# A decoder layer in fp32: gate and up of the ffn wholly by seven products, with new raw buffers and queued sums

## The chip, the cores and the metric

The kernel runs on one core of a Trainium2 chip, in one launch. The metric is the device time of the launch in microseconds (us), the median of three runs. TensorE (PE) multiplies; its weight loads are listed apart as PEld and overlap the products. VectorE (DVE), ScalarE (ACT) and GpSimd (POOL) are the elementwise engines, and SyncE (SP) issues most transfers from HBM.

## The reference

One layer of a decoder for 256 tokens of width 2048, all in float32: a half-step ffn, a mixer of attention and gated linear attention, cross attention into 256 memory tokens, and a second half-step ffn. What matters here are the two ffns, of hidden width 5632:

```python
def swiglu(h, w_gate, w_up, w_down):
    return (jax.nn.silu(h @ w_gate) * (h @ w_up)) @ w_down

x = x + 0.5 * swiglu(rms_norm(x, ffn1_norm), ...)      # the same again at the end, with ffn2's weights
```

## The kernel before, in words

**Numbers.** An fp32 product is made of three fp32r matmuls: each operand is split into a rounded high part and the rest, and high x high, high x low and low x high are summed in one PSUM bank. A weight tile of 128 x 4 x 512 floats (1 MB) is loaded raw by SP, ScalarE casts it to `wh` in two halves (L157 or L201), DVE subtracts for `wl` (L158 or L202), and PE multiplies. The pools of `wh` and `wl` have four halves each (`WB`), so DVE runs at most four halves ahead of PE. x stands transposed in four chunks `xT[c]` of 4 K-tiles, each as a high and a low tile.

**The ffn.** The hidden width is cut in 11 blocks f of 512 columns. For each f, gate and up are formed (two token tiles of 128 each, so four PSUM banks), silu(gate) * up goes to `sg` on DVE (L216, as every `urgent` operation), it is transposed by PE into hT (`turn`, L387; `hTh` on ScalarE, `hTl` on DVE L304), and `down` multiplies it by four 512-column chunks of w_down, 24 matmuls each, banks `dn`, adding to the residual `xs`. The downs of f-1 are put between the steps of f.

**Seven products.** f=0 forms gate and up plainly, 96 matmuls each. From f=1 on, gate and up of one f are treated together as a 2 x 2 block product: x's two token tiles by two K-parts, times K-parts by (gate, up). `seven` (L257) computes it with seven block products for eight, in the banks Y, Z, X and R: sums of weight blocks, T = gate + gate', T + up and so on, are formed on raw tiles by DVE (`add`, L207) or by an accumulating transfer that POOL issues (`add_hbm`, L211), and the differences of x blocks (`xf`, `d`, `Fh`, `Fl`) are formed once for each ffn by `x_differences` (L400) and kept. Before, chunks 0 and 1 are one pair of blocks (four K-tiles), the two halves of chunk 2 are a second pair (two K-tiles), and chunk 3 is plain: 84 + 42 + 48 = 174 matmuls for each f. The differences are put off by `later(DIFF, ...)` into up of f=0; the rest of them comes at the change to f=1.

**Order.** Each engine runs its instructions in one order, which the framework sets from the order in the code and from priorities (`high_priority`): a larger number goes earlier as far as its operands and buffers allow. Loads have `LPRI`, splits and sums `WPRI`, the steps that free a bank `FPRI`.

**Buffers.** Raw tiles come from a pool for the whole kernel (4 x 1 MB), and in the ffns from two more (`r`, 3 x 1 MB, and `q`, 4 halves). `enter` closes the pools of a stage and opens those of the next. A buffer of the pool for the whole kernel passes from one stage to the next by itself; one in a pool of the stage starts when the old pool is done.

Of the kernel before, what the change touches and what calls it, by code (L numbers as in the profile page):

```python
# [8 lines left out]
F32 = mybir.dt.float32  # L9
# [7 lines left out]
P = 128  # L17
# [13 lines left out]
WARM = 10  # L31
# [12 lines left out]
UF = 18  # L44
UM = 34
SB = 7
RB = 4
RX = 3
RQ = 4
DIFF = 1  # L50
# [3 lines left out]
def layer_kernel(ctx: ExitStack, tc: tile.TileContext, A: dict, out: bass.AP):  # L54
# [25 lines left out]
    def enter_ffn():  # L80
        enter(2, down=2, u=UF, r=RX, q=RQ)

# [3 lines left out]
    def raw_tile(kind="raw"):  # L86

        if kind == "raw":
            return wp.tile([P, 4, 512], F32, tag="raw", name="raw", bufs=RB)
        return stage[kind].tile([P, 2 if kind == "q" else 4, 512], F32, tag=kind, name="raw")  # L90
# [45 lines left out]

    def wgroup(W, c, g, fine=None):
# [4 lines left out]
        with tc.high_priority(WPRI):  # L142
            if wload:
                raw = wload.pop(0)
            else:
                raw = wp.tile([P, kn, n], F32, tag="raw", name="raw", bufs=RB)
                SY.dma_start(raw, W[c, g])
        for h in range(2):
            with tc.high_priority(WPRI):
                wh = wp.tile([P, m, n], F32R, tag="wh", name="wh", bufs=WB)  # L150
                wl = wp.tile([P, m, n], F32R, tag="wl", name="wl", bufs=WB)
                for i in range(m if fine else 1):
# [5 lines left out]
                    V.tensor_sub(wl[:, d], src, wh[:, d].bitcast(F32))  # L158
# [29 lines left out]
    def load(src, kind="raw"):  # L188
        with tc.high_priority(ahead[0]):
            raw = raw_tile(kind)  # L190
            SY.dma_start(raw, src)
        return raw

    def parts(raw, n=4):

        for h in range(n // 2):
            with tc.high_priority(WPRI):
# [4 lines left out]
                V.tensor_sub(wl, src, wh.bitcast(F32))  # L202
            yield [(2 * h + kk, wh[:, kk], wl[:, kk]) for kk in range(2)]

    def add(dst, src):
        with tc.high_priority(WPRI):
            V.tensor_add(dst, dst, src)  # L207

    def add_hbm(dst, src):
        with tc.high_priority(WPRI):  # L210
            G.dma_start(dst, src, accum_op=ALU.add)  # L211
# [13 lines left out]
    def product(bank, form, raw, start, n):  # L225

        for h, half in enumerate(parts(raw, n)):
            mms(bank, form, half, start and h == 0, h == n // 2 - 1)
# [8 lines left out]
    PAIRS = {"22-21": ((1, 1), (1, 0)), "12-21": ((0, 1), (1, 0)), "22-12": ((1, 1), (0, 1)),  # L237
             "21-11": ((1, 0), (0, 0)), "11-12": ((0, 0), (0, 1))}

    def difference(x, name, n, home=None):  # L240

        a, b = PAIRS[name]
        with tc.high_priority(WPRI):
            d = W2([P, n, P], "d")
            V.tensor_sub(d, x[a], x[b])
            if home:
                hi, lo = home
            elif n == 4:
                hi, lo = (U([P, 4, P], F32R, nm) for nm in ("Fh", "Fl"))
            else:  # L250
                both = U([P, 4, P], F32R, "Fhl")
                hi, lo = both[:, 0:2], both[:, 2:4]
            SC.copy(hi, d)
            V.tensor_sub(lo, d, hi.bitcast(F32))
        return hi, lo

    def seven(blocks, ld, last, rest):  # L257
# [22 lines left out]
        for i, (n, kinds, F, A12, A21) in enumerate(blocks):  # L280
            b22.append(load(ld(i, 1, 1), kinds[3]))
            add(T[i], b22[i])
            product(R, A12, T[i], i == 0, n)
        urgent(V.tensor_sub, X, R, sw)
# [6 lines left out]
        urgent(V.tensor_sub, R, R, sv)  # L291
        for i, (n, kinds, F, A12, A21) in enumerate(blocks):
            product(X, F["22-12"], b22[i], False, n)
        plain((R, X), (rest(0), rest(1)), load(last(1)), (1, 0))
        yield "down"
        for i, (n, kinds, F, A12, A21) in enumerate(blocks):
            product(Y, F["11-12"], b12[i], False, n)
        yield "down"
        plain((Y, Z), (rest(0), rest(1)), load(last(0)), (0, 1))
        return Y, Z, R, X  # L300
# [817 lines left out]
```

## Time and profile before

| | |
|---|---|
| Median of three runs | 1919.39 us (1917.73 to 1922.42) |
| The profiled execution's own time | 1917.25 us |
| Its span | 1915.5 us |
| Granted TensorE clock, mean | 0.998 |
| PE busy | 1892.8 us (99%) |
| DVE busy | 1471.9 us (77%) |
| ACT busy | 1288.9 us (67%) |
| POOL busy | 94.8 us (5%) |

The span runs from the first to the last instruction of the profiled execution; its own time has some 2 us around it. An engine's busy time is a mean over stages: the loop of the ffns takes about seven tenths of the span and is alike in each period from f=2 on. Matmul records overlap, so their pitch (start to start) is what one costs, not their length.

### The profile page before, as it was taken

To read this page: it belongs to the slowest core of one execution; us is meant where nothing else is said; L and a number is where in the kernel's file an instruction comes from. 1 tells how busy PE (TensorE), PEld (TensorE's weight loads), DVE (VectorE), ACT (ScalarE), POOL (GpSimd) and SP (SyncE) were. 2 spreads that over 40 slices of the span, in tenths; PEclk is the share of its full clock that TensorE was granted. 3 is DMA by queue.
4 is the path that set the end of the run, shared out by engine and by line. 5 is a ranking of instruction groups with operands and counts; after the bars stand their busy time and mean duration, and the time that the engine had idled before them with its cause. 6 is when DMAs were issued, how large, how long until landed. Compare 5 with 4: busy or idle time off the path is not lost.

```text
span 1915.5 us, 22853 instructions
## 1 busy us (share of the span) xinstructions
PE 1892.8 (99%) x8640; PEld 1566.4 (82%) x8640; DVE 1471.9 (77%) x1499; ACT 1288.9 (67%) x1695; POOL 94.8 (5%) x101
## 2 busy tenths in 40 slices
PE   8899999999999999999999999999999999999999
PEld 6688888888888878778888889877888888888887
DVE  6987888788878865546785655898788878887884
ACT  6567777777777776444576545656777777777775
POOL 2000000000000000002220000000000000000000
PEclk9999999999999999999999999999999999999999
DMA  9577666776577444445466554747766677657743
GB/s 370 199 240 245 220 205 223 242 242 214 214 247 259 132 176 151 173 155 194 173 225 214 178 190 161 271 171 234 247 220 205 223 242 242 210 216 248 250 142 110
DMA packets 69211, 405.76 MB, mean 212 GB/s; under 512 B 7755, under 2 KB 8907, under 8 KB 28012
## 3 DMA queue, kind: packets, MB, share of 16 engines
q1 hardware_dynamic: 62188, 370.74, 52.2%
q0 software_dynamic: 5760, 31.46, 8.8%
q10 hardware_dynamic: 1152, 2.10, 0.3%
q8 instruction: 67, 1.10, 0.2%
q14 instruction: 44, 0.36, 0.1%
HBM read 402.17 MB, written 2.10 MB: 211 GB/s over the span
## 4 chain that ended last, share of the span: by engine, by line
PE 96%; DVE 2%; DMA 1%; ACT 1%; issue 0%; SPq 0%; DVEq 0%; ACTq 0%
PE acc L221 13%; PE acc L222 13%; PE acc L223 13%; PE acc L166 9%; PE acc L167 9%; PE acc L168 9%; PE dn L166 8%; PE dn L168 8%; PE dn L167 8%; DMA raw<-in_ffn_w_gate_dram 1%; PE tp L387 1%; DVE wl L202 1%; PE tp L344 1%; DVE raw L207 0%; PE dsp L697 0%
## 5 line engine op out<-in xcount | busy, mean ns | idle before, releaser
L201 ACT CAST wh<-raw 128x1024 fp32r<-128x1024 f32 x500 | 517.3, 1051 | 275.5 <-PE dn L168 103.8
L202 DVE TENSOR_TENSOR wl<-raw,wh 128x1024 fp32r<-128x1024 f32 x500 | 594.1, 1220 | 114.9 <-ACT wh L201 114.5
L158 DVE TENSOR_TENSOR wl<-raw,wh 128x1024 fp32r<-128x1024 f32 (+1 forms) x370 | 447.9, 1223 | 186.1 <-ACT wh L157 183.9
L157 ACT CAST wh<-raw 128x1024 fp32r<-128x1024 f32 (+1 forms) x370 | 384.9, 1048 | 205.3 <-PE acc L168 159.7
L222 PE MATMUL acc<-wl,xTh 128*128 128x512 f32 x800 | 313.2, 391 | 7.3 <-DVE wl L202 7.3
L221 PE MATMUL acc<-wh,xTh 128*128 128x512 f32 x800 | 312.7, 391 | 2.0 <-ACT wh L201 1.9
L223 PE MATMUL acc<-wh,xTl 128*128 128x512 f32 x800 | 312.7, 391 | 0.0
L166 PE MATMUL dn<-wh,hTh 128*128 128x512 f32 x704 | 274.7, 391 | 1.6 <-ACT hTh L303 1.1
L167 PE MATMUL dn<-wl,hTh 128*128 128x512 f32 x704 | 274.5, 390 | 0.5 <-DVE wl L158 0.5
L168 PE MATMUL dn<-wh,hTl 128*128 128x512 f32 x704 | 274.6, 390 | 0.0
L207 DVE TENSOR_TENSOR raw<-raw 128x2048 f32<-128x2048 f32 (+1 forms) x120 | 209.2, 1756 | 65.6 <-DMA raw<-in_ffn_w_gate_dram 64.1
L166 PE MATMUL acc<-wh,xTh 128*128 128x512 f32 x544 | 216.5, 398 | 6.4 <-ACT wh L157 6.4
L167 PE MATMUL acc<-wl,xTh 128*128 128x512 f32 x544 | 213.7, 393 | 0.0
L168 PE MATMUL acc<-wh,xTl 128*128 128x512 f32 x544 | 213.5, 392 | 0.0
L222 PEld LDWEIGHTS acc<-wl,xTh 128*128 128x128 f32 x800 | 150.8, 188 | 40.3 <-DVE wl L202 9.1
L221 PEld LDWEIGHTS acc<-wh,xTh 128*128 128x128 f32 x800 | 150.8, 189 | 34.1 <-ACT wh L201 2.8
L223 PEld LDWEIGHTS acc<-wh,xTl 128*128 128x128 f32 x800 | 150.8, 189 | 31.1
L166 PEld LDWEIGHTS dn<-wh,hTh 128*128 128x128 f32 x704 | 132.1, 188 | 30.9 <-ACT hTh L303 1.6
L167 PEld LDWEIGHTS dn<-wl,hTh 128*128 128x128 f32 x704 | 132.2, 188 | 28.2 <-DVE wl L158 1.1
L168 PEld LDWEIGHTS dn<-wh,hTl 128*128 128x128 f32 x704 | 132.2, 188 | 28.2 <-DVE hTl L304 0.9
L166 PEld LDWEIGHTS acc<-wh,xTh 128*128 128x128 f32 x544 | 103.0, 189 | 28.7 <-ACT wh L157 7.1
L167 PEld LDWEIGHTS acc<-wl,xTh 128*128 128x128 f32 x544 | 103.0, 189 | 21.6 <-DVE wl L158 0.9
(287 smaller groups left out, 2163.5 us busy)
## 6 DMA issues: line engine op xcount, KB each, us to landing
raw<-in_ffn_w_down_dram SPq DMA_DIRECT2D x88, 1024.0 KB, 6.5
raw<-in_ffn_w_up_dram SPq DMA_DIRECT2D x68, 1024.0 KB, 7.0
raw<-in_ffn_w_gate_dram SPq DMA_DIRECT2D x65, 1024.0 KB, 5.9
raw<-in_w_in_dram SPq DMA_DIRECT2D x48, 1024.0 KB, 4.8
raw<-in_ffn_w_gate_dram SPq DMA_DIRECT2D x44, 512.0 KB, 5.5
raw<-in_ffn_w_up_dram SPq DMA_DIRECT2D x40, 512.0 KB, 7.4
raw<-in_ffn_w_gate_dram POOLq DMA_DIRECT2D x20, 1024.0 KB, 8.7
raw<-in_w_out_dram SPq DMA_DIRECT2D x16, 1024.0 KB, 4.9
```

Source lines behind the costliest of these rows:

```text
L157: SC.copy(wh[:, d], src)
L158: V.tensor_sub(wl[:, d], src, wh[:, d].bitcast(F32))
L166: PE.matmul(acc[t], lh, wh, start=first and i == 0, stop=False, **kw)
L167: PE.matmul(acc[t], lh, wl, start=False, stop=False, **kw)
L168: PE.matmul(acc[t], ll, wh, start=False, stop=last and i == len(half) - 1, **kw)
L201: SC.copy(wh, src)
L202: V.tensor_sub(wl, src, wh.bitcast(F32))
L207: V.tensor_add(dst, dst, src)
L221: PE.matmul(bank, hi[:, k], wh, start=start and i == 0, stop=False, skip_group_check=True)
L222: PE.matmul(bank, hi[:, k], wl, start=False, stop=False, skip_group_check=True)
L223: PE.matmul(bank, lo[:, k], wh, start=False, stop=stop and i == len(half) - 1, skip_group_check=True)
L344: PE.transpose(tp[:, j], src[:, t, j * P:(j + 1) * P], ident)
```

## The change

- `Blocks` replaces `x_differences`: chunks 0 and 1 are the first pair, chunks 2 and 3 the second, each of four K-tiles. A difference is formed when it is first asked for: those of the first pair in f=1, those of the second in f=2.
- `seven` takes one pair in f=1 (and chunks 2 and 3 plainly, 84 + 96 = 180 matmuls) and two pairs from f=2 on (168).
- From f=2 on, the second pair's first sum, T[1] = gate + gate', is formed by an accumulating transfer instead of by DVE; POOL issues three of these in a period where it issued two. DVE's sums in a period are five of 128 x 2048 where they were three of 128 x 2048 and three of 128 x 1024; splits are 36 halves where they were 33.
- `add` is placed behind the fourth-last split made so far (`issue_after(splits[-WB].ins)`); accumulating transfers are kept in order among each other.
- One pool `raw` of nine 1 MB buffers in the ffns and of five between them replaces the three pools; it belongs to the stage. R is formed after the third product of Y.
- `fill`: all down banks start from 2 x the residual, also in f=1, where a dummy matmul opens each bank; so DVE's residual update of f=0's downs becomes one on ScalarE.
- At the start, twenty warm-up matmuls (on a piece of `xs`) come first on PE; before, ten stand behind 31 of the real ones. The first four pieces of x are scaled on POOL instead of on ScalarE, and ScalarE casts the first four weight pieces ahead of those of x.

```diff
-WARM = 10
+WARM = 20
-UF = 18
-UM = 34
-SB = 7
-RB = 4
-RX = 3
-RQ = 4
+UF = 20
+UM = 36
+SB = 6
+RF = 9
+RM = 5
...
     def add(dst, src):
+        with tc.high_priority(WPRI), tc.issue_after(splits[-WB].ins):
+            V.tensor_add(dst, dst, src)
...
+    def seven(F, ld, rest, hbm):
+        Y, Z, X, R = [pa.tile([P, 512], F32, tag="acc", name="acc") for _ in range(4)]
+        N = range(len(F))
+        T, b12, b21 = [], [], []
+        for i in N:
+            T.append(load(ld(i, 0, 0)))
+            if i in hbm:
+                add_hbm(T[i], ld(i, 1, 0))
+                b21.append(load(ld(i, 1, 0)))
             else:
+                b21.append(load(ld(i, 1, 0)))
+                add(T[i], b21[i])
+            product(Y, F[i].A21, T[i], i == 0)
         urgent(SC.copy, Z, Y)
         yield "turn"
+        for i in N:
+            product(Z, F[i]["22-21"], b21[i], False)
         yield "down"
+        for i in N:
+            b12.append(load(ld(i, 0, 1)))
             add(T[i], b12[i])
+            product(Y, F[i]["12-21"], T[i], False)
...
-                first, second = ("22-21", "12-21", "22-12"), ("21-11", "11-12")
-                later(DIFF, lambda: x_differences(x4, 4, F4, first))
-                later(DIFF + 2, lambda: x_differences(x2, 2, F2, first))
+                F = [Blocks(0), Blocks(2)]
...
+                n = 1 if f == 1 else 2
+                rest = [([x_block(t, c) for t in range(TT)], lambda col, c=c: W[col][f, c]) for c in range(2 * n, NC)]
+                steps = seven(F[:n], lambda i, row, col: W[col][f, 2 * i + row], rest, () if first or n == 1 else (1,))
...
-        if n == 1:
-            SC.activation(xr[:, 0], xr[:, 0], AF.Copy, scale=gain[:, g0 + k0:g0 + k0 + 1])
-        else:
-            G.tensor_tensor(xr, xr, gain[:, g0 + k0:g0 + k0 + n].unsqueeze(2).broadcast_to([P, n, S]), op=ALU.mult)
+        G.tensor_tensor(xr, xr, gain[:, g0 + k0:g0 + k0 + n].unsqueeze(2).broadcast_to([P, n, S]), op=ALU.mult)
...
-    enter(4, u=UM)
+    enter(4, raw=RM, u=UM)
```

Three places of the order. First DVE at the change to f=2 of ffn1, from the gate product on; `wl` are splits, `raw<-raw` sums, `hTl` the low half of the transposed h, `xf`, `d` and `Fl` the sums, difference and low half of x blocks. Before:

```order
L216 SCALAR_TENSOR_TENSOR sg<-acc,r_344,sg 128x512 x2
L202 TENSOR_TENSOR wl<-raw,wh 128x1024 x3
L207 TENSOR_TENSOR raw<-raw 128x1024
L304 TENSOR_TENSOR hTl<-tp,hTh 128x512 x2
L158 TENSOR_TENSOR wl<-raw,wh 128x1024 x2
L202 TENSOR_TENSOR wl<-raw,wh 128x1024 x2
L207 TENSOR_TENSOR raw<-raw 128x2048
L202 TENSOR_TENSOR wl<-raw,wh 128x1024
L207 TENSOR_TENSOR raw<-raw 128x1024
L202 TENSOR_TENSOR wl<-raw,wh 128x1024 x3
L158 TENSOR_TENSOR wl<-raw,wh 128x1024 x2
```

And of the changed kernel:

```order
L221 SCALAR_TENSOR_TENSOR sg<-acc,r_350,sg 128x512 x2
L201 TENSOR_TENSOR wl<-raw,wh 128x1024 x4
L207 TENSOR_TENSOR raw<-raw 128x2048
L336 TENSOR_TENSOR hTl<-tp,hTh 128x512
L201 TENSOR_TENSOR wl<-raw,wh 128x1024
L336 TENSOR_TENSOR hTl<-tp,hTh 128x512
L263 TENSOR_TENSOR xf<-xTh_239,xTl_240 128x512 x2
L263 TENSOR_TENSOR xf<-xTh_279,xTl_280 128x512 x2
L157 TENSOR_TENSOR wl<-raw,wh 128x1024
L272 TENSOR_TENSOR d<-xf 128x512
L157 TENSOR_TENSOR wl<-raw,wh 128x1024
L275 TENSOR_TENSOR Fl<-d,Fh 128x512
```

The sums and the first difference of chunks 2 and 3 now stand between hTl and the down projection's second split, and a full sum stands ahead of hTl.

The second place is DVE in a later period, from the four splits after the gate product on. Before:

```order
L202 TENSOR_TENSOR wl<-raw,wh 128x1024 x3
L304 TENSOR_TENSOR hTl<-tp,hTh 128x512
L158 TENSOR_TENSOR wl<-raw,wh 128x1024
L304 TENSOR_TENSOR hTl<-tp,hTh 128x512
L158 TENSOR_TENSOR wl<-raw,wh 128x1024
L202 TENSOR_TENSOR wl<-raw,wh 128x1024 x2
L207 TENSOR_TENSOR raw<-raw 128x1024
L207 TENSOR_TENSOR raw<-raw 128x2048
L202 TENSOR_TENSOR wl<-raw,wh 128x1024
L207 TENSOR_TENSOR raw<-raw 128x1024
L202 TENSOR_TENSOR wl<-raw,wh 128x1024 x3
```

And of the changed kernel:

```order
L201 TENSOR_TENSOR wl<-raw,wh 128x1024 x4
L336 TENSOR_TENSOR hTl<-tp,hTh 128x512
L201 TENSOR_TENSOR wl<-raw,wh 128x1024
L336 TENSOR_TENSOR hTl<-tp,hTh 128x512
L157 TENSOR_TENSOR wl<-raw,wh 128x1024 x2
L207 TENSOR_TENSOR raw<-raw 128x2048 x2
L201 TENSOR_TENSOR wl<-raw,wh 128x1024 x4
L157 TENSOR_TENSOR wl<-raw,wh 128x1024 x2
L201 TENSOR_TENSOR wl<-raw,wh 128x1024 x2
L207 TENSOR_TENSOR raw<-raw 128x2048
L201 TENSOR_TENSOR wl<-raw,wh 128x1024
L207 TENSOR_TENSOR raw<-raw 128x2048
```

Two full sums stand back to back behind the first down's splits, and all are of 128 x 2048.

The third place is SP at the entry to ffn2, with what each load waits for; `w_o` is the output projection of cross attention. Before:

```order
L147 DMA raw<-in_xattn_w_o_dram 128x2048 [waits DMAHW7_49,DVE_49]
L147 DMA raw<-in_xattn_w_o_dram 128x2048 [waits DMAHW0_49,DVE_49]
L147 DMA raw<-in_ffn_w_gate_dram 128x2048 [waits DMAHW1_49,DVE_49]
L147 DMA raw<-in_ffn_w_gate_dram 128x2048 [waits DMAHW2_49,DVE_49]
L147 DMA raw<-in_ffn_w_gate_dram 128x2048 [waits DMAHW3_49,DVE_49]
L147 DMA raw<-in_ffn_w_gate_dram 128x2048 [waits DMAHW4_49,DVE_49]
L147 DMA raw<-in_ffn_w_up_dram 128x2048 [waits DMAHW5_49,DVE_49]
L191 DMA raw<-in_ffn_w_gate_dram 128x2048 [waits PE_49]
```

And of the changed kernel:

```order
L146 DMA raw<-in_xattn_w_o_dram 128x2048 [waits DMAHW2_49,DVE_49]
L146 DMA raw<-in_xattn_w_o_dram 128x2048 [waits DMAHW3_49,DVE_49]
L146 DMA raw<-in_ffn_w_gate_dram 128x2048 [waits DMAHW4_49,DMAHW5_49,DMAHW0_49,DMAHW6_49,DVE_49,DMAHW7_49,PE_49,Pool_49]
L146 DMA raw<-in_ffn_w_gate_dram 128x2048 x3
L146 DMA raw<-in_ffn_w_up_dram 128x2048 x4
L190 DMA raw<-in_ffn_w_gate_dram 128x2048 [waits DMAHW1_49]
```

The first gate load waits for PE (its last matmul of w_o), DVE and POOL, where it waited for DVE's split out of the same buffer only; the next three follow it with no wait of their own.

## Rows read from the trace of the kernel before

**Rows 1.** The page: busy times, and the chain that ended last by engine.
```profile
PE 1892.8 (99%) x8640; PEld 1566.4 (82%) x8640; DVE 1471.9 (77%) x1499; ACT 1288.9 (67%) x1695; POOL 94.8 (5%) x101
...
PE 96%; DVE 2%; DMA 1%; ACT 1%; issue 0%; SPq 0%; DVEq 0%; ACTq 0%
```
**Rows 2.** Waits of PE, whole run: us in total, times, longest.
```profile
PE acc L222 <- DVE wl L202: 7.3, 4, 5.4
PE acc L166 <- ACT wh L157: 6.4, 1, 6.4
```
**Rows 3.** Windows: length, busy time (records) by engine, PEclk, DMA share, GB/s.
```profile
196.37:258.51 62.14, 62.14 (x281) 51.57 (x279) 52.23 (x46) 45.94 (x56) 1.72 (x2) 1.00 0.68 228
63.42:68.28 4.86, 4.86 (x11) 3.81 (x12) 4.86 (x5) 2.21 (x3) 0.00 (x0) 0.50 0.00 0
1190.00:1230.00 40.00, 40.00 (x195) 33.56 (x194) 33.34 (x44) 24.14 (x39) 0.69 (x1) 1.00 0.63 233
1281.10:1283.10 2.00, 1.24 (x4) 0.84 (x5) 2.00 (x2) 2.00 (x3) 0.00 (x0) 1.00 0.00 0
```
**Rows 4.** Timeline of PE in a period: start, length, line, tiles [idle before].
```profile
239.31 0.39 PE L221 MATMUL acc<-wh,xTh 128*128 128x512 f32 x1
...
243.16 0.39 PE L223 MATMUL acc<-wh,xTl 128*128 128x512 f32 x1
```
**Rows 5.** Timeline of PE at the start.
```profile
6.39 0.80 PE L166 MATMUL acc<-wh,xTh 128*128 128x512 f32 x1 [6.39 <-ACT wh L157]
...
17.56 2.39 PE L520 MATMUL wps<-idle 128*128 128x128 f32 x20
19.70 0.48 PE L167 MATMUL acc<-wl,xTh 128*128 128x512 f32 x1
```
**Rows 6.** Timeline of SP: weight loads at the start, and ffn2's first.
```profile
2.58 0.43 SPq L133 DMA_DIRECT2D raw<-in_ffn_w_gate_dram  x1
...
4.48 0.43 SPq L133 DMA_DIRECT2D raw<-in_ffn_w_gate_dram  x1
...
1186.79 18.45 SPq L147 DMA_DIRECT2D raw<-in_ffn_w_gate_dram  x4
```
**Rows 7.** Timeline of ACT: a weight cast at the start, and a full one.
```profile
7.62 0.62 ACT L157 CAST wh<-raw 128x512 fp32r<-128x512 f32 x1 [0.44 <-DMA raw<-in_ffn_w_gate_dram]
...
1209.96 1.05 ACT L157 CAST wh<-raw 128x1024 fp32r<-128x1024 f32 x1
```
**Rows 8.** Timeline of PE at ffn1's change from f=0 to f=1.
```profile
63.42 0.80 PE L222 MATMUL acc<-wl,xTh 128*128 128x512 f32 x1 [5.41 <-DVE wl L202]
...
69.37 0.51 PE L222 MATMUL acc<-wl,xTh 128*128 128x512 f32 x1 [0.56 <-DVE wl L202]
...
71.47 0.50 PE L221 MATMUL acc<-wh,Fh 128*128 128x512 f32 x1 [0.66 <-ACT acc L216]
```
**Rows 9.** Timeline of DVE: differences, splits, a sum, hTl.
```profile
42.77 1.89 DVE L245 TENSOR_TENSOR d<-xf 128x512 f32<-128x512 f32 x3
...
209.39 3.49 DVE L202 TENSOR_TENSOR wl<-raw,wh 128x1024 fp32r<-128x1024 f32 x3
...
236.71 2.29 DVE L207 TENSOR_TENSOR raw<-raw 128x2048 f32<-128x2048 f32 x1 [3.06 <-DMA raw<-in_ffn_w_gate_dram]
238.92 2.35 DVE L202 TENSOR_TENSOR wl<-raw,wh 128x1024 fp32r<-128x1024 f32 x2
...
259.92 0.69 DVE L304 TENSOR_TENSOR hTl<-tp,hTh 128x512 fp32r<-128x512 f32 x1
```
**Rows 10.** Timeline of PE: transposes ahead of ffn2, and ffn2's f=1.
```profile
1205.04 1.91 PE L344 MATMUL tp<-ident,x 128*128 128x128 f32 x16
...
1281.10 0.50 PE L221 MATMUL acc<-wh,xTh 128*128 128x512 f32 x1 [1.92 <-ACT wh L201]
```
**Rows 11.** Transfers: KB each, median us from issue to landing.
```profile
raw<-in_ffn_w_gate_dram SPq DMA_DIRECT2D x65, 1024.0 KB, 5.9
...
raw<-in_ffn_w_gate_dram POOLq DMA_DIRECT2D x20, 1024.0 KB, 8.7
```

More of the change, by code (lines that the diff above doesn't have):

```diff
@@ L80, in enter_ffn, with raw_tile @@
     def enter_ffn():
-        enter(2, down=2, u=UF, r=RX, q=RQ)
+        enter(2, down=2, raw=RF, u=UF)
     def U(shape, dt, name):
         return stage["u"].tile(shape, dt, tag="u", name=name)
[L86 to L90, printed above, removed]
+    def raw_tile():
+        return stage["raw"].tile([P, 4, 512], F32, tag="raw", name="raw")
     enter_ffn()
@@ L186, in layer_kernel, with load, parts @@
     ahead = [LPRI]
-    def load(src, kind="raw"):
+    def load(src):
         with tc.high_priority(ahead[0]):
-            raw = raw_tile(kind)
+            raw = raw_tile()
             SY.dma_start(raw, src)
         return raw
-    def parts(raw, n=4):
-        for h in range(n // 2):
+    def parts(raw):
+        for h in range(2):
             with tc.high_priority(WPRI):
@@ L210, in add_hbm @@
         with tc.high_priority(WPRI):
-            G.dma_start(dst, src, accum_op=ALU.add)
+            if adds:
+                with tc.issue_after(adds[-1].ins):
+                    adds.append(G.dma_start(dst, src, accum_op=ALU.add))
+            else:
+                adds.append(G.dma_start(dst, src, accum_op=ALU.add))
     def urgent(op, *args, **kw):
@@ L223, in mms, with product @@
             PE.matmul(bank, lo[:, k], wh, start=False, stop=stop and i == len(half) - 1, skip_group_check=True)
-    def product(bank, form, raw, start, n):
-        for h, half in enumerate(parts(raw, n)):
-            mms(bank, form, half, start and h == 0, h == n // 2 - 1)
+    def product(bank, form, raw, start):
+        for h, half in enumerate(parts(raw)):
+            mms(bank, form, half, start and h == 0, h == 1)
             tick()
@@ L278, in seven @@
         sw = W2([P, 512], "sw")
         urgent(SC.copy, sw, Y)
[L280 to L284, printed above, removed]
         yield "down"
-        for i, (n, kinds, F, A12, A21) in enumerate(blocks):
-            product(Y, F["21-11"], b12[i], False, n)
+        for i in N:
+            product(Y, F[i]["21-11"], b12[i], False)
@@ L290, in seven @@
         urgent(SC.copy, sv, Y)
[L291 to L294, printed above, removed]
+        b22 = []
+        for i in N:
+            b22.append(load(ld(i, 1, 1)))
+            add(T[i], b22[i])
+            product(R, F[i].A12, T[i], i == 0)
+        urgent(V.tensor_sub, X, R, sw)
+        urgent(V.tensor_sub, R if rest else sv, R, sv)
         yield "down"
[L296 to L297 removed]
+        for i in N:
+            product(X, F[i]["22-12"], b22[i], False)
+        for forms, src in rest:
+            plain((R, X), forms, load(src(1)), (1, 0))
         yield "down"
[L299 to L300 removed]
+        for forms, src in rest[:-1]:
+            plain((Y, Z), forms, load(src(0)), (1, 0))
+        for i in N:
+            product(Y, F[i]["11-12"], b12[i], False)
+        for forms, src in rest[-1:]:
+            plain((Y, Z), forms, load(src(0)), (0, 1))
+        return Y, Z, R if rest else sv, X
     def split_from_psum(hi, lo, ps):
@@ L378, in ffn @@
         hT = {}
-        F4, F2 = {}, {}
         def turn(f, hs):
@@ L419, in down @@
         def down(f, c):
-            acc = filled.pop() if filled else [stage["dn"].tile([P, 512], F32, tag="dn", name="dn") for _ in range(TT)]
+            acc = filled.pop()
             if last and f == NF - 1 and c == NC - 1:
@@ L518, in layer_kernel @@
     wps = PM([P, P], "wps")
-    for i in range(WARM):
-        PE.matmul(wps, idle, idle, start=True, stop=True)
+    with tc.high_priority(100000):
+        idle = xs[0][:, 0, 0:P]
+        V.memset(idle, -0.5)
+        for i in range(WARM):
+            PE.matmul(wps, idle, idle, start=True, stop=True)
     ident = con.tile([P, P], F32, name="ident")
```

121 lines of the change are left out of this document (53 added, 68 removed).

## The prediction

> **What bounds the kernel now.** I read the page's busy times and its chain first, then TensorE's waits over the whole run, then one period of the ffn loop as a window, and last the places where TensorE does wait. TensorE (PE) is busy 99% of the span and carries 96% of the chain that ends last [rows 1]. All its waits together come to under 20 us, and two of them are most of that: 6.4 us at the start, and 7.3 us for VectorE's (DVE) splits, of which one wait alone is 5.4 us [rows 2]. One period of the loop, from one turn of h to the next, is 62.14 us, and PE is busy in all of it at full clock; DVE is busy for 52.23 us of it, 84%, ScalarE for 45.94 [rows 3]. A 512-column matmul takes 0.39 us but starts every 0.2265 us: 18 of them start from 239.31 to 243.16, 17 steps in 3.85 us [rows 4]. A period's 270 matmuls at that pitch and 8 transposes make the 62.1 us. So a matmul that goes saves its pitch, as long as nothing else becomes late, and DVE is the next engine that can.
>
> **A. Matmuls.** With all 16 K-tiles in two seven-product blocks, a period from f=2 on has 2 x 84 = 168 matmuls for gate and up, where 84 + 42 + 48 = 174 stood: 6 fewer, 6 x 0.2265 = 1.36 us. Nine such periods in each ffn, 18 in all: -24.5 us. In f=1 only the first block is a pair and two chunks are plain: 84 + 96 = 180, 6 more, twice: +2.7. Four matmuls that open the down banks: +0.9. Together **-20.9**; bounds -24.5 and -18, since this is a count at a measured pitch.
>
> **B. Start.** Before, ten warm-up matmuls of 128 columns stand in the middle of real work, from 17.56 to 19.70 [rows 5]: 2.1 us that go. Now twenty stand ahead of it. In exchange the first real matmul starts later: ScalarE casts four weight pieces before x. In the run before, the second piece was issued at 2.58 and its cast began at 7.62, as soon as it was there, 5.0 us later [rows 6, 7]; the fourth, issued at 4.48, would be there at 9.5, two casts later it is 10.5, and 24 matmuls at full clock end at 16.0. Before, the 24th ended seven pitches ahead of 17.56, at 16.0 as well, though the first started at 6.39. Twenty warm ones at half clock need 2 x 2 x 2.14 = 8.6 us, over by then. **-2.1** (-2.4; +2.4 if the clock were still halved).
>
> **C. ffn1, f=1.** Before, PE waits 5.41 us for DVE, which forms the differences of x there, and then 0.56 and 0.66 [rows 8]; after the first of these the granted clock is 0.50 for 4.86 us [rows 3], which costs half of that. In all 6.6 + 2.4 = 9.0. Now only the differences of chunks 0 and 1 are formed here, behind the first splits. A split's pitch on DVE is 1.13 us (three in 3.49), a full add's 2.21 (236.71 to 238.92), a 512-column difference or hTl 0.60 (three in 1.89) [rows 9]. Between DVE's gate product and the low half of the difference stand splits, two hTl, four sums, one difference: lined up against PE's matmuls this leaves 5.7 us idle, with a halved clock up to 8.1. **-2.2** (-3.4 to -1). In ffn2 the same place cost little before, 1.92 us at its longest, and the clock stayed at 1.00 [rows 3, 10]; now down matmuls stand between. **0** (-1 to +1).
>
> **E. f=2 of both ffns: a new wait.** The differences of chunks 2 and 3 are formed here, where before nothing of the kind stood. Behind the turn DVE has in its queue: a full add 2.21, hTl 0.6, split 1.13, hTl 0.6, four sums 2.4, split 1.13, difference 0.6, split 1.13, low half 0.6 = 10.4, and it starts on them 0.9 us late, so the low half is there 11.3 us after Y ends. PE has in the meantime 8 transposes and 12 matmuls of the first block, then two of the down projection, 4.0 us; the third needs the split at 9.0. So it idles about 4.9, then 0.8 and 0.5: 6.2 us. Queued behind this on DVE are the next difference and the add for the third product; PE's 29 matmuls by then (6.6 us) cover them. Clock: after 5.41 idle it was halved, after 1.92 it was not; 4.9 is nearer the former, and half clock here costs only 1.3 us, since it overlaps the two smaller waits. I take half of that: 2 x 6.8 = **+13.6** (8 to 18.5).
>
> **F. Periods from f=3 on (16).** PE needs 264 x 0.2265 + 0.9 = 60.7 us. DVE now has 36 splits for 33, 5 full adds for three full and three half: 3 x 1.13 + 2 x 2.21 - 3 x 1.15 = +4.4 - so 52.2 becomes 56.6, 93%. (A half add is taken as a split's size and price.) ScalarE has three more casts of 1.05 [rows 7]: 49, covered. The accumulating transfers go from two to three a period and land in 8.7 us against 5.9 for a plain one [rows 11]; the new one has its buffer free about half a period ahead. What I line up by hand is DVE's queue against PE's: the splits used first are ahead of the adds, and it comes out even at two places, where two adds stand back to back, short by 0 to 0.2 us. **+3** (0 to 24, the upper end if 1.5 us a period are lost).
>
> The Trainium skill, in Perfetto Trace Analysis, section Identifying the Most-Contended Engine, says that a matmul's busy share misleads and that PE is to be judged by its weight loads, the other engines by occupancy. By that rule DVE (84%) is already on a level with PE (weight loads 51.57 of 62.14, 83%) and the added DVE work would lengthen the period; at an unchanged share of 84% it would be 56.6 / 0.84 = 67 us instead of 60.7, some 100 us more over 16 periods: the far end of the third rival below. The trace doesn't bear the rule out here: in the window PE leaves no gap at a pitch that doesn't vary, while DVE shows idle time of 3.06 us ahead of one add [rows 3, 9].
>
> **G. Stage changes.** Before, the raw buffers outlive a stage: ffn2's first four gate loads issue from 1186.79 on, and PE is busy for 40.00 of 40 us around the border [rows 3, 6]. Now the pool is closed and opened again, and the first of these loads waits for the last matmul of the output projection. From there: a landing (5.9 us in the median for w_gate) and a cast of 1.05 [rows 7, 11], against sixteen transposes, 1.9 us [rows 10], and a little more. **+4.5** (1 to 8, the latter with a halved clock). Into the mixer the reopened pool waits for ffn1's last split; 36 matmuls are queued behind that, 8.2 us, against 7 of load and cast: 0 (0 to 2).
>
> Sum: -20.9 - 2.1 - 2.2 + 0 + 13.6 + 3 + 4.5 = **-4.1**. The profiled execution took 1917.25 us (span 1915.5), so 1913.1; the median of the runs is 1919.39, which would give 1915.3. I say 1914.
>
> **Rivals.**
> 1. The matmuls decide. If DVE gets through f=2 with half the wait (6 us in both together), the period has no stall and ffn2's first load is hidden: -20.9 - 2.1 - 2.2 + 6.5 = -18.7, about 1899. For it: a DVE that had 3 us of slack in places [rows 9]. Against it: the queue is in order, and it stood so at 63.42.
> 2. The clock. After 5.41 us of idle PE ran at half clock [rows 3, 8]; four places now have waits of that order (both f=2, f=1, ffn2's entry). If it is halved fully at each, and nothing overlaps: 4 x 2.4 less the 1.3 already counted, +8, about 1921, no difference. The skill's page TensorE: Matmul & The Clock Gate, section on HAM oscillation, describes this: a wait lets the clock fall and the matmuls behind it start cold each time. The trace agrees at 63.42 and not at 1281.10, where the clock stayed.
> 3. DVE becomes the bound of the loop. In its in-order queue an add waits for an accumulating or a plain transfer, and four splits queue behind it; at 93% it has no time to catch up within the period. With 1.5 us a period instead of 0.2: 16 x 1.3 = +21, and another 2 at each f=2: 1913 + 25 = 1938, slower. It decides from 0.9 us a period on, where the forecast is 0.3% above before. For it: 93%, and the 3.06 us that DVE waits for a transfer before an add [rows 9]. Against it: that wait cost PE nothing, and the adds now stand behind the splits PE needs first.
>
> **How the numbers follow.** A measurement of this kernel tells about 0.3% (5.8 us) from no change, so the borders are 1913.6 and 1925.2. My forecast, 1905 to 1921, has 0.42, of which 0.23 lies under the border. The first rival has 0.22, the second 0.16 (same), the third 0.20 (slower, with little in the same band). Faster 0.46, same 0.34, slower 0.20. The range reaches into both outer rivals: 1897 to 1932; the forecast's own is 1905 to 1921.
>
> **What will show it.** A period from turn to turn of 60.7 to 61 us from f=3 on, with PE full; then A and F hold. At f=2 of each ffn a wait of about 5 us in the down matmuls, released by DVE's split, with sums and a difference ahead of it; at 1210 or so a wait for ffn2's first gate load and cast of 4 to 5 us. A wait behind L207 in every period would show rival 3. If f=2's waits are under 3 us, E is wrong, and rival 1 nearer.

## The result, and the profile after

The changed kernel takes 1928.60 us in the median of five runs (1925.46 to 1929.24), the kernel before 1919.18 beside it: 1.0045 times as long, interval 1.0030 to 1.0060. So it is slower by 0.45%, 9 us, where 5 us less were forecast. The time lies in the wide range (1897 to 1932) but above the forecast's own (1905 to 1921), and the sign is wrong. The profiled execution took 1927.92 us (span 1926.1, mean granted clock 0.992; before 1915.5 and 0.998).

The page's busy times and its chain by engine:

```profile
PE 1892.1 (98%) x8568; PEld 1553.9 (81%) x8568; DVE 1533.6 (80%) x1507; ACT 1346.3 (70%) x1771; POOL 112.6 (6%) x121
...
PE 78%; DVE 11%; DMA 5%; ACT 3%; issue 2%; SPq 0%; ACTq 0%; POOLq 0%
```

Against [rows 1], PE has fewer matmuls and the same busy time in a longer span: what they saved has turned into waits and slower matmuls. DVE's 11% of the chain doesn't mean that DVE bounds 11% of the time: a wait of PE hands the chain to DVE, and it stays there as long as DVE runs back to back. How much PE waits stands in its waits over the whole run (us in total, times, longest):

```profile
PE dn L166 <- DVE wl L157: 10.2, 3, 4.7
PE acc L165 <- ACT wh L156: 3.7, 1, 3.7
PE acc L226 <- DVE acc L221: 3.5, 2, 1.8
PE acc L226 <- ACT Fh L274: 3.3, 1, 3.3
PE acc L165 <- ACT xTh L356: 2.9, 1, 2.9
```

The long wait for DVE of [rows 2] is gone; a wait for ScalarE's cast of a weight stands at ffn2's entry now and not at the start, and the four others listed are new. In order of time, windows of f=2 of ffn1, the part of it behind its wait, a period of the loop, the last one, the stretch between the ffns, the part of that behind its wait, and f=2 of ffn2 (length, busy time and records of PE, PEld, DVE, ACT, POOL; granted clock, DMA share, GB/s):

```profile
132.93:202.82 69.89, 64.94 (x273) 52.06 (x272) 64.33 (x61) 51.53 (x64) 2.58 (x3) 0.95 0.70 226
141.85:148.68 6.83, 6.44 (x14) 4.58 (x15) 6.75 (x8) 2.28 (x3) 0.00 (x0) 0.50 0.50 167
...
509.13:570.13 61.00, 61.00 (x273) 50.28 (x272) 56.31 (x48) 48.50 (x59) 2.60 (x3) 1.00 0.78 259
631.13:689.03 57.90, 56.13 (x249) 45.61 (x248) 51.09 (x44) 43.27 (x53) 1.73 (x2) 1.00 0.53 164
689.03:1270.58 581.55, 576.69 (x2778) 479.11 (x2777) 354.29 (x486) 330.94 (x512) 50.26 (x45) 0.99 0.51 186
1220.46:1227.29 6.83, 6.20 (x14) 4.42 (x15) 4.95 (x5) 3.79 (x5) 0.00 (x0) 0.50 1.01 427
...
1341.33:1411.82 70.49, 65.19 (x273) 51.98 (x272) 64.04 (x61) 51.33 (x64) 2.58 (x3) 0.95 0.70 224
```

And of the kernel before: f=2 of ffn1, its last period, and the stretch between the ffns:

```profile
134.00:196.21 62.21, 62.21 (x280) 51.56 (x278) 51.98 (x46) 46.23 (x56) 1.72 (x2) 1.00 0.68 228
...
631.42:689.78 58.36, 58.36 (x261) 48.11 (x260) 44.73 (x41) 41.40 (x51) 1.72 (x2) 1.00 0.52 161
689.78:1264.40 574.62, 574.06 (x2783) 478.76 (x2782) 366.81 (x516) 335.73 (x523) 49.69 (x45) 1.00 0.52 187
```

The loop does what was wanted: 61.00 us with PE full, against 62.14 [rows 3]. The f=2 periods, alike with the loop before, are now 9 us longer than it, at a clock of 0.95, and in each of the two 14 matmuls behind the wait run at half clock.

With the whole span cut at the turns of h, each stretch's change splits into its count of 512-column matmuls, at 0.2267 us, and the rest. "Forecast" is the prediction's term for that rest.

| stretch | before | after | by count | rest | forecast |
|---|---|---|---|---|---|
| start to the first turn | 56.53 | 58.13 | +1.36 | +0.25 | B -2.1 |
| ffn1, f=1 | 77.47 | 74.79 | +1.81 | -4.5 | C -2.2 |
| f=2, both ffns | 124.43 | 140.38 | -2.7 | +18.7 | E +13.6 |
| f=3 to 9, both | 870.31 | 856.38 | -19.0 | +5.1 | F +3 (all 16) |
| f=10, both | 116.71 | 115.81 | -5.4 | +4.5 | in F |
| between the ffns | 574.62 | 581.54 | -1.4 | +8.3 | G +4.5 |
| ffn2, f=1 | 67.07 | 70.76 | +4.5 | -0.85 | D 0 |
| tail | 28.33 | 28.35 | 0 | 0 | 0 |

The counts sum to -20.9 and the rests to +31.5, together the 10.6 us by which the spans differ.

PE at these places (timeline: start, length, line, tiles, count, idle before and what ended it), in order of time: the start, f=2 of ffn1, its last period, the entry to ffn2:

```profile
1.06 6.75 PE L533 MATMUL wps<-x 128*128 128x128 f32 x40 [1.06 <-DVE mhalf L524]
10.66 0.50 PE L165 MATMUL acc<-wh,xTh 128*128 128x512 f32 x1 [2.86 <-ACT xTh L356]
12.26 0.80 PE L167 MATMUL acc<-wh,xTl 128*128 128x512 f32 x1 [0.40 <-DVE xTl L357]
...
142.21 0.79 PE L166 MATMUL dn<-wl,hTh 128*128 128x512 f32 x1 [4.69 <-DVE wl L157]
...
666.87 0.47 PE L226 MATMUL acc<-wh,Fh 128*128 128x512 f32 x1 [1.76 <-DVE acc L221]
...
1216.05 1.26 PE L373 MATMUL tp<-ident,x 128*128 128x128 f32 x8 [0.51 <-DVE xg L375]
1221.05 1.22 PE L165 MATMUL acc<-wh,xTh 128*128 128x512 f32 x2 [3.75 <-ACT wh L156]
```

And DVE, whose queue makes the wait at 142.21:

```profile
129.34 4.74 DVE L201 TENSOR_TENSOR wl<-raw,wh 128x1024 fp32r<-128x1024 f32 x4 [0.18 <-ACT wh L200]
133.99 2.29 DVE L207 TENSOR_TENSOR raw<-raw 128x2048 f32<-128x2048 f32 x1
136.19 0.69 DVE L336 TENSOR_TENSOR hTl<-tp,hTh 128x512 fp32r<-128x512 f32 x1
136.80 1.22 DVE L201 TENSOR_TENSOR wl<-raw,wh 128x1024 fp32r<-128x1024 f32 x1
137.93 0.69 DVE L336 TENSOR_TENSOR hTl<-tp,hTh 128x512 fp32r<-128x512 f32 x1
138.53 2.49 DVE L263 TENSOR_TENSOR xf<-xTh,xTl 128x512 f32<-128x512 f32 x4
140.93 1.22 DVE L157 TENSOR_TENSOR wl<-raw,wh 128x1024 fp32r<-128x1024 f32 x1
```

DVE waits for nothing from 129.34 on. It reaches the down projection's first split at 140.93, and PE starts again when that ends; ahead of it stand a full add (2.29), where a half one stood before, and the sums of x (2.49), which are new.

### The profile page after: what moved, and what is told of

Its sections match the earlier page's. It is cut to its first block, busy times and chain, and to the rows that moved or that the text cites. A ratio compares the mean times of both kernels' runs of the same rounds, so it can differ in the third digit from the quotient of the medians.

```text
span 1926.1 us, 22714 instructions
## 1 busy us (share of the span) xinstructions
PE 1892.1 (98%) x8568; PEld 1553.9 (81%) x8568; DVE 1533.6 (80%) x1507; ACT 1346.3 (70%) x1771; POOL 112.6 (6%) x121
## 4 chain that ended last, share of the span: by engine, by line
PE 78%; DVE 11%; DMA 5%; ACT 3%; issue 2%; SPq 0%; ACTq 0%; POOLq 0%
PE acc L227 10%; PE acc L226 9%; PE acc L228 9%; PE acc L165 9%; PE acc L167 9%; PE acc L166 9%; PE dn L165 6%; PE dn L166 6%; PE dn L167 6%; DVE wl L201 5%; DMA raw<-in_ffn_w_gate_dram 5%; DVE raw L207 3%; DVE wl L157 2%; ACT wh L200 1%; ACT wh L156 1%
## 5 line engine op out<-in xcount | busy, mean ns | idle before, releaser
L201 DVE TENSOR_TENSOR wl<-raw,wh 128x1024 fp32r<-128x1024 f32 x548 | 649.2, 1219 | 104.7 <-ACT wh L200 102.5
L227 PE MATMUL acc<-wl,xTh 128*128 128x512 f32 x672 | 263.9, 393 | 1.0 <-DVE wl L201 0.8
L228 PE MATMUL acc<-wh,xTl 128*128 128x512 f32 x672 | 261.8, 390 | 0.0
L226 PE MATMUL acc<-wh,xTh 128*128 128x512 f32 x672 | 261.3, 389 | 0.0
L165 PE MATMUL acc<-wh,xTh 128*128 128x512 f32 x544 | 216.4, 398 | 6.6 <-ACT wh L156 3.7
L207 DVE TENSOR_TENSOR raw<-raw 128x2048 f32<-128x2048 f32 x96 | 217.9, 2283 | 0.0
L167 PE MATMUL acc<-wh,xTl 128*128 128x512 f32 x544 | 213.6, 393 | 0.4 <-DVE xTl L357 0.4
L166 PE MATMUL acc<-wl,xTh 128*128 128x512 f32 x544 | 213.4, 392 | 0.0
L226 PE MATMUL acc<-wh,Fh 128*128 128x512 f32 x456 | 183.1, 402 | 6.9 <-DVE acc L221 3.5
L227 PE MATMUL acc<-wl,Fh 128*128 128x512 f32 x456 | 180.8, 396 | 0.0
L228 PE MATMUL acc<-wh,Fl 128*128 128x512 f32 x456 | 180.1, 395 | 0.0
L227 PEld LDWEIGHTS acc<-wl,xTh 128*128 128x128 f32 x672 | 126.1, 188 | 33.5 <-DVE wl L201 7.8
L226 PEld LDWEIGHTS acc<-wh,xTh 128*128 128x128 f32 x672 | 126.2, 188 | 26.4
```

Of the source, the lines that this page charges most:

```text
L165: PE.matmul(acc[t], lh, wh, start=first and i == 0, stop=False, **kw)
L166: PE.matmul(acc[t], lh, wl, start=False, stop=False, **kw)
L167: PE.matmul(acc[t], ll, wh, start=False, stop=last and i == len(half) - 1, **kw)
L201: splits.append(V.tensor_sub(wl, src, wh.bitcast(F32)))
L226: PE.matmul(bank, hi[:, k], wh, start=start and i == 0, stop=False, skip_group_check=True)
L227: PE.matmul(bank, hi[:, k], wl, start=False, stop=False, skip_group_check=True)
```

## The experiments

All are edits of the changed kernel; ratios are to the kernel before, which stands at 1 beside the changed kernel's 1.0045.

**1. The differences of the second pair formed a period earlier.** In f=1 `later` asks for them; f=2 then finds them ready.

```diff
+                if f == 1:
+                    later(18, F[1].whole)
+                    later(22, lambda: F[1]["22-21"])
+                    later(28, lambda: F[1]["12-21"])
                 steps = seven(F[:n], ...
```

> The changed kernel, with the x sums of chunks 2 and 3 and their first two differences formed late in f=1 instead of at the turn of f=2. Theory W (the wait at f=2): the period of f=2 falls from 69.9 and 70.5 us to 61 to 62 in both ffns, its granted clock is 1.00 throughout, f=1 grows by at most 2 us, and the time falls by 14 to 18 us, to 1911 to 1915. Rival D (VectorE is short of time in the whole loop, and f=2 is only where it shows): the work is the same, so the wait moves to f=1 or later; the sum of f=1 to f=3 falls by less than 5 us and the time stays above 1922.

Measured: 1913.06 us, 0.9968 (0.9957 to 0.9979). f=2 of ffn1:

```profile
132.67:195.47 62.80, 61.51 (x273) 50.10 (x272) 59.31 (x53) 50.00 (x62) 2.58 (x3) 1.00 0.78 251
```

62.80 and 62.77 us where 69.89 and 70.49 stood, at full clock, with 1.29 us of idle left, and f=1 no longer for it (74.40). The two periods stay 0.8 above the 61 to 62 that were expected. That is 14.8 us by the windows, 15.5 by the medians: theory W holds, the place of the loss is shown, and it alone turns the change from slower to faster. It doesn't yet part the wait from the clock.

**2. Only the clock held up.** Twenty matmuls with weights of zero, which add nothing, are put on PE ahead of the wait, between the two blocks of Z (`hold` is 20 at f=2 and else 0). They cost PE time, so this can only gain by what half clock costs.

```diff
         for i in N:
             product(Z, F[i]["22-21"], b21[i], False)
+            for _ in range(hold if i == 0 else 0):
+                PE.matmul(Z, zero, xT[0][0][:, 0:2]..., start=False, stop=False)
```

> The changed kernel, with twenty matmuls by a zero weight tile (which add zero to Z) between the first and second block of Z in f=2 of each ffn, 4.5 us of TensorE's time inside the wait of 4.7 us. Theory K (the halved clock is a cost of its own behind the wait): the granted clock stays 1.00 there, the 14 matmuls at half clock go, and each f=2 period falls by 2 to 3 us, from 69.9 and 70.5 to about 67.5; time 1922 to 1925. Rival W alone (VectorE's chain sets the end, the slower matmuls run in its shadow): the periods change by less than 0.7 us.

Measured: 1923.88 us, 1.0025 (1.0016 to 1.0035).

```profile
132.61:199.41 66.80, 66.10 (x293) 53.94 (x292) 63.92 (x61) 51.06 (x64) 2.57 (x3) 1.00 0.73 236
```

In the two f=2 periods no matmul is at half clock any more: 3.1 us less here and 3.7 in ffn2 (66.79 for 70.49), a little more than the 2 to 3 expected. By the medians it is less, 4.7 us for both: the profiled execution is the fastest of the ten, 1920.36 us. DVE's queue is as before, so the wait is not shorter: 20 x 0.2267 = 4.5 us of filler stand where 4.95 us of idle were, and 0.70 are left. Theory K holds: half clock by itself costs 2.4 us (medians) to 3.7 (windows) at each of the two places; the prediction had priced it at 0.65.

**3. Twenty or thirty-two warm-up matmuls.** `WARM` 20 becomes 32.

> The changed kernel, with 32 warm-up matmuls for 20. Theory K: TensorE is busy to about 10.4 us, no half clock from 12.1 to 15.6, and ffn1's first turn starts at 56.0 to 56.8 instead of 58.13. Rival: the first matmuls wait for VectorE's low halves of x anyway, and the first turn stays within 0.5 us of 58.1.

Measured, a single run: 1924.47 us, span 1922.7, 3.4 less than the profile after. The five runs of the changed kernel spread over 3.8 us by themselves, so the total shows little; the trace says more.

```profile
11.22 0.50 PE L165 MATMUL acc<-wh,xTh 128*128 128x512 f32 x1 [1.05 <-ACT xTh L356]
...
12.82 0.50 PE L167 MATMUL acc<-wh,xTl 128*128 128x512 f32 x1 [0.87 <-DVE xTl L357]
```

No half clock at the start. The first turn comes at 58.74 with five more matmuls done by then, 57.6 for the same work: about half a microsecond, not one to two. The expectation for the start is missed, because x's parts come later in this run: the first matmul starts at 11.22 instead of 10.66, and PE waits 0.87 for DVE's low half against 0.40 at 12.26. This place also differs between runs of the same code: in experiment 6 below, with twenty, the first turn came at 56.80 and the clock didn't fall.

The other part comes in f=1, whose rest falls by 2.3, with no half clock there either; at the second turn 2.8 us are gained. But there the edit also changed PE's order: twenty matmuls of the down projection now stand ahead of the first one with `Fh`, where two stood, and cover its wait. The profile after, and this run:

```profile
65.80 0.80 PE L226 MATMUL acc<-wh,Fh 128*128 128x512 f32 x1 [3.29 <-ACT Fh L274]
```
```profile
67.56 0.40 PE L226 MATMUL acc<-wh,Fh 128*128 128x512 f32 x1
```

So most of this gain is put down to the order, by the trace, and not to the warmer start. It is there in every trace: the three with 32 (this one and experiments 7 and 8) have this order and their second turn at 130.14 to 130.57, the profile after and experiments 1, 2, 5 and 6, with twenty, at 131.19 to 133.23.

**4. Some raw buffers kept across the stage border.** Five of nine come from a pool for the whole kernel, four from the ffn's, taken in a fixed turn of nine.

```diff
+        n = nraw[0]
+        nraw[0] = (n + 1) % RF
+        if n < RM or "raw" not in stage:
+            return wp.tile([P, 4, 512], F32, tag="raw", name="raw", bufs=RM)
         return stage["raw"].tile([P, 4, 512], F32, tag="raw", name="raw")
```

> The changed kernel, with five of the nine raw buffers in a pool for the whole kernel and four in the ffns' own, used in the same turn of nine; so ffn2's first five loads wait for one buffer each. Theory G (the reopened pool): the wait of 3.75 us for ffn2's first weight cast goes, the clock is 1.00 there, and the stretch from ffn1's last turn to ffn2's first, 581.5 us, falls by 6 to 8 us; time 1920 to 1923. Rival: the load is late for the transfers themselves or for the transposes of x, and the stretch falls by less than 2 us.

Measured: 1987.61 us, 1.0354 (1.0335 to 1.0373). Three periods of the loop, and the stretch between the ffns:

```profile
202.28:275.95 73.67, 67.34 (x286) 54.00 (x284) 60.56 (x51) 53.39 (x64) 2.60 (x3) 0.95 0.72 226
275.95:339.54 63.59, 61.85 (x274) 50.10 (x273) 56.03 (x48) 48.36 (x59) 2.59 (x3) 1.00 0.77 248
339.54:398.08 58.54, 58.53 (x261) 48.00 (x260) 52.74 (x44) 43.54 (x54) 2.60 (x3) 1.00 0.77 254
723.52:1297.71 574.19, 573.17 (x2778) 477.10 (x2777) 353.47 (x486) 330.35 (x512) 49.83 (x45) 1.00 0.51 184
```

The border does what was expected: 574.19 for 581.54, full clock, 7.4 us. The time misses its expectation because the edit changed a second thing: a load must now take the next buffer in turn, not one that is free. A period has 12 loads, so the pattern of 9 repeats every third period, and so do the lengths, on average 65.3 us instead of 61.2; PE waits 36.1 us in all, seven times, for the cast of a late tile. That was not foreseen, and the total says nothing about the border.

**5. The sums not queued behind the splits.** `add` without `issue_after`.

```diff
-        with tc.high_priority(WPRI), tc.issue_after(splits[-WB].ins):
+        with tc.high_priority(WPRI):
             V.tensor_add(dst, dst, src)
```

> The changed kernel, with a sum on VectorE queued by its priority alone and no longer behind the fourth-last split. Theory Q (the sums' place in VectorE's queue keeps the loop's period at 61): sums of 2.2 us come ahead of splits that TensorE needs at once, each period from f=3 on loses 0.5 us or more against 61.0 to 61.6, and the time grows by 8 us or more, above 1936. Rival: with the splits up to four halves ahead the place of a sum does not matter; periods within 0.2 us of the changed kernel's, time 1925 to 1931.

Measured: 1995.84 us, 1.0408 (1.0392 to 1.0424), 67 us more than the changed kernel. A period; in it, on DVE, one sum with the subtraction behind it that forms the bank X (X = R - sw); and PE there:

```profile
334.66:402.81 68.15, 64.75 (x273) 52.19 (x272) 56.76 (x48) 48.58 (x59) 2.59 (x3) 0.95 0.72 231
```
```profile
373.72 2.29 DVE L207 TENSOR_TENSOR raw<-raw 128x2048 f32<-128x2048 f32 x1 [4.58 <-DMA raw<-in_ffn_w_gate_dram]
375.93 0.69 DVE L221 TENSOR_TENSOR acc<-acc,sw 128x512 f32<-128x512 f32 x1
```
```profile
376.76 0.47 PE L226 MATMUL acc<-wh,Fh 128*128 128x512 f32 x1 [1.85 <-DVE acc L221]
378.39 0.79 PE L227 MATMUL acc<-wl,Fh 128*128 128x512 f32 x1 [1.16 <-DVE wl L201]
```

A sum stands 4.58 us at the head of DVE's queue for its transfer; the subtraction and four splits stand behind it, and PE waits twice; 14 matmuls of the period then run at half clock. DVE's work in the period is the same 56 us as in the changed kernel. Theory Q holds, far more strongly than its price: in this kernel the new place in the queue is worth three times what the matmuls are. It is the third rival's mechanism, at 3 to 7 us a period, kept out by where the sums stand.

**6. More work for DVE, fewer accumulating transfers.** T[1]'s first sum goes back to DVE: `hbm` is empty also from f=2 on.

> The changed kernel, with T[1]'s first sum on VectorE in every period instead of by an accumulating transfer: six sums a period, 2.2 us more, VectorE at 97% of 60.7. Theory D (VectorE has no time left): the periods from f=3 on grow by 0.5 to 2 us each, the time by 8 to 30 us, to 1936 to 1960. Rival: the sum falls into VectorE's idle time, periods within 0.2 us, time 1925 to 1931.

Measured: 1928.44 us, 1.0056 (1.0040 to 1.0071), not distinguished from the changed kernel.

```profile
324.24:385.50 61.26, 61.26 (x274) 50.25 (x272) 58.26 (x49) 48.44 (x59) 1.71 (x2) 1.00 0.72 240
```

DVE is busy for 58.26 of 61.26 us, 95%, and PE has no gap. Theory D falls: DVE's share isn't what decides in the loop. The added accumulating transfer, part of the change, buys nothing measurable.

**7. Three edits together.** Experiment 1, `WARM = 32`, and three downs, not two, between the steps of f=10, so that PE has matmuls while DVE gets through its eight splits there:

```diff
-                    elif f < NF - 1 or len(todo) > 2:
+                    elif f < NF - 1 or len(todo) > 1:
```

> The changed kernel with three edits: the early differences of e1_early (-15.5), 32 warm-up matmuls as in e4_warm32 (-2 to -4), and three of the four downs put between the steps of f=10 instead of two, so that one stands between R and the product on X. Theory L (X waits for VectorE's subtraction because no matmuls stand between): the wait of 1.76 us in each last period goes, -3.5; time 1904 to 1909, faster than before by 0.5 to 0.8%. Rival: with only one down left for the end, TensorE waits there for silu and the gate product instead, and the last period and what follows it stay as long; time 1909 to 1913.

Measured: 1905.96 us, 0.9938 (0.9926 to 0.9951). The last period of ffn1:

```profile
622.38:678.21 55.83, 55.82 (x250) 45.75 (x249) 51.91 (x44) 43.61 (x53) 1.72 (x2) 1.00 0.55 170
```

55.83 for 57.90, without the wait of 1.76, twice. With experiment 1's 15.5, these 4.2 and the 2.8 of experiment 3, 22.5 us were to be had, and 22.6 came. So close a match is in part chance: by the spans the stretch between the ffns is 1.6 us shorter (7 matmuls at half clock behind its wait instead of 14), and f=3 to 9 are 1.2 us longer.

**8. One raw buffer kept across the border, held by name.** Experiment 7, and one buffer of the ffns' nine lives through the whole kernel: it takes ffn2's first gate tile and, in each period, w_down's tile of chunk 2 (`one` is set for these alone), so no load of the loop depends on a turn.

```diff
+            elif one:
+                raw = wp.tile([P, 4, 512], F32, tag="raw1", name="raw", bufs=1)
+                SY.dma_start(raw, W[c, g])
```

> As e8_three, and one raw buffer of the nine lives through the whole kernel: ffn2's first gate tile is loaded into it ahead of the border, and one down a period uses it; eight are left in the ffns, four between. Theory G: ffn2's first cast no longer waits, the clock stays 1.00 there, the stretch from ffn1's last turn to ffn2's first falls by 4 to 7 us below e8_three's; the loop stays at 61 to 61.3; time 1898 to 1904. Rival B (buffers): with eight buffers for eleven loads, or in a fixed turn as in e2_keep, the loop's periods grow by 1 us or more, and the time is not below e8_three's.

Measured: 1899.39 us, 0.9902 (0.9888 to 0.9915): faster than before by 1.0% and than the changed kernel by 1.4%, by the ratios. A period of the loop, and the stretch between the ffns:

```profile
378.08:439.10 61.02, 61.02 (x274) 50.28 (x273) 56.31 (x48) 48.52 (x59) 2.59 (x3) 1.00 0.80 259
679.35:1252.91 573.56, 573.27 (x2777) 477.06 (x2776) 352.45 (x485) 330.04 (x512) 49.54 (x45) 1.00 0.51 188
```

The border's waits and its half clock are gone, the loop is untouched: what experiment 4 left open. Against the kernel before beside it, 1918.34, that is 19 us, near A's 20.9; the shorter f=1 and the start are in it too.

## Why the prediction was wrong, point by point

**A, the matmuls: right.** 20.9 us by count and pitch. The forecast sum of the losses was 16.8 and they came to 31.5; the difference of 14.7 is what follows.

**E, f=2: the mechanism right, the size wrong (+5.1), the largest single miss.** Wait, releaser and the work ahead of it are as worked out (4.69 for 4.9, all idle 4.95 and 5.30 for 6.2). The step that failed is "half clock here costs only 1.3 us, since it overlaps the two smaller waits. I take half of that". Experiment 2 parts the two: at full clock the period would lose 5.6 us to the loop's 61.2 (4.5 of filler, 0.70 of idle and 0.4), a little less than the 6.2; with the clock halved it loses 8.7. The smaller waits that were to absorb the slow matmuls are 0.70, not 1.3, and 14 matmuls at 0.43 us instead of 0.2267 are 2.8 by themselves. Nor was it an even chance: the clock fell in all ten f=2 periods of the five traces that have this wait, with 11 to 14 matmuls at half clock. Put alone into the forecast, this miss moves it from -4.1 to +1.0; but with E as forecast and all else as measured the kernel would still be 5.5 us slower, so the sign doesn't hang on E alone.

**G, the border: the mechanism right, the size at the bound (+3.8).** The load waits for the output projection's last matmul and PE waits 0.51 us for x's last transposes and 3.75 for the first weight cast, near the 4.5 taken. The load isn't alone in it. It was issued at 1214.74 and landed after 5.1 us, at about the moment when ScalarE was through with the casts of x's last blocks, and the weight's cast followed without idle time:

```profile
1218.75 1.21 ACT L378 CAST xTh<-xg 128x512 fp32r<-128x512 f32 x2 [1.51 <-DVE xg L375]
1219.95 1.99 ACT L156 CAST wh<-raw 128x1024 fp32r<-128x1024 f32 x2
```

So by this trace the load and the end of x's preparation come out even, and the prediction had only the first. With the load ahead of the border, in experiments 4 and 8, products of the earlier x blocks stand between the last transposes and cover both. Here too 14 matmuls then run at half clock, 2.8 us; behind the same wait it was 6 to 14 in the seven traces that have it. The upper bound of 8 had held a halved clock. About 1.2 us of the 8.3 isn't placed; experiments 4 and 8 give back 7.4 to 8.

**F, the loop: near for f=3 to 9 (+5.1 in 14 periods, 0.4 each for at most 0.2), wrong for the last (+4.5).** The prediction counted f=10 as a period like the others. It has fewer matmuls beside DVE's work, and DVE stands like this:

```profile
656.95 9.16 DVE L201 TENSOR_TENSOR wl<-raw,wh 128x1024 fp32r<-128x1024 f32 x8
666.03 0.69 DVE L221 TENSOR_TENSOR acc<-acc,sw 128x512 f32<-128x512 f32 x1
```

Eight splits, 9.16 us, ahead of the subtraction that forms X, for which PE waits 1.76 at 666.87. Three downs between the steps cover it (experiment 7).

**B, the start: wrong by 2.4.** The first real matmul came nearly when it was forecast, 10.66 for 10.5. "Twenty warm ones at half clock need ... 8.6 us, over by then" failed: they were over at 7.81, after 6.75 us, and PE then idled 2.86 until 10.66 with the clock falling at 12.1. The time was taken from the wrong side: a warm-up that ends early leaves a wait behind it. Eight matmuls at half clock are 1.6 us, and the wait for xTl is 0.40. Experiment 3 takes the half clock away; its larger part, in f=1, goes with another order.

**C and D: 2.3 and 0.85 better.** What f=1 of ffn1 still loses came out as said: its rest of 7.92 less 0.9 for eight transposes is 7.0, forecast 9.0 - 2.2 = 6.8. The sum fits better than its parts, and that is luck: 4.0 us of idle and ten matmuls at half clock stand where 5.7 of idle were lined up. It was the loss before that was undercounted, 11.5 for 9.0. In that one are 7.3 us of waits and 12 matmuls at half clock, 2.4; the other 1.8 isn't placed.

**The rivals.** The second, the clock, was the one that came: it fell at the start, in f=1, at both f=2 and at ffn2's entry. The trace after has 60 matmuls at half clock there, before it had 12: 48 x 0.2 = 9.6 us. The rival had 4 x 2.4 = 9.6 as well, the forecast 1.3 of it; that the time is 8 us above the rival's 1921 is the last periods' wait, the start and the loop, which it took from the forecast. Five terms came out dearer than forecast, by 17.9 us (f=2 5.1, the last periods 4.2, the border 3.8, f=3 to 9 2.5, the start 2.3), and C and D gave 3.2 back. Of the 17.9, the clock is about half (4.3 more at f=2 by experiment 2's windows, 2.8 at the border and 1.6 at the start by the count of slow matmuls). That the wide range still held the time is luck: it reached to 1932 for the third rival, which didn't come.

The Trainium skill, in TensorE: Matmul & The Clock Gate, section HAM oscillation, says that a wait that is long enough makes the matmuls behind it cold, every time it comes; the ten f=2 periods agree. The wait of 1.92 us at 1281.10, which the prediction counted against the page, doesn't speak against it, since the page has long waits in mind. The same page of the Trainium skill, in its part on the clock gate, holds the ramp to be under 1% of a usual span and a cold count not worth fitting. It speaks of the ramp at a kernel's start, which is 1.6 of the 9.6 us here; all 9.6 are 0.5% of the span, and as much as the whole slowdown.

The first rival (DVE gets through f=2) fell with E. The third fell as a forecast for this kernel: the loop keeps its 61 us. By the occupancy that Perfetto Trace Analysis of the Trainium skill, section Identifying the Most-Contended Engine, goes by, DVE would have come first: 92% of a period after, against 82% for PE's weight loads (the page names the share of peak FLOPs for PE as well, which wasn't worked out). Experiment 6 shows that 95% leaves PE without a gap; experiment 5 shows the reverse, 3 to 7 us lost a period at an unchanged amount of DVE work. Where an operation stands in the queue decides here, not the share.

**What stays open.** Why the same start keeps the clock in one run and loses it in another, and the unplaced 1.2 us at the border. That the start gains so little from 32 warm-up matmuls is put down to x's later parts by the trace alone; no run took that wait away. Nor did a run change PE's order in f=1 alone.

## What to carry to other kernels

Work that is formed when it is first asked for lands where its user already waits; ask for it a period earlier, where PE has cover, and look at the last trip of a loop for itself, since it has less cover than the others. A wait of PE of 3 to 5 us has to be priced with the half clock behind it, here 2.4 to 3.7 us more at f=2, which overlap gave back only in small part, and 1 to 3 at the border, depending on the run. On an engine with one queue, put an operation that waits for a transfer behind those that PE needs next, before counting its busy share; and keep one raw buffer outside the pools of a stage, so that the next stage's first load is not behind the last matmul of this one.

## What was not expected of the hardware

- The twenty warm-up matmuls (40 records) took 6.75 us from 1.06 on, and those from 10.66 on ran at full clock; it fell to half at 12.1, 4.3 us after the warm-up's end, though four matmuls of 512 columns had run by then.

```profile
12.14:15.56 3.42, 3.30 (x8) 2.62 (x9) 3.42 (x6) 2.96 (x4) 1.93 (x2) 0.50 1.04 417
```

- The clock fell in or behind idle times of 2.86 (start), 3.29 (f=1), 4.69, 3.75 and 4.68 us in the profile after, and didn't after 1.92 before [rows 10] and 1.76 after. At the start of experiments 4 and 6, with the same twenty warm-up matmuls and waits of 2.80 and 2.44 us, it held; in the other three traces with twenty, with waits of 3.59 to 4.20, it fell. No one length divides them: it fell behind 2.38 (f=1) and 1.80 us (the last period of ffn2) in experiment 4, and in experiment 5 at 377.47 behind waits of 1.85 and 1.16 close together, while at 1560 there 1.77 and 1.15 left it at full.
- PE's idle time in a stretch doesn't bound its loss: at f=2, 4.95 us of idle went with 8.7 us lost against the loop's 61.2.
